# Sharing the first copies, moving adaLN steps off the first two heads, reordering the first FFN weights, spreading two merges, and updating x by ScalarE and GpSimd in a conditioned decoder trunk

## The chip, the core and the metric

The kernel runs on one core of one Trainium2 chip. Its five instruction streams are called by the profile's names: PE (TensorE), DVE (VectorE), ACT (ScalarE), POOL (GpSimd) and SP (the queue from which nearly all DMAs are issued). The metric is the device time of one execution in microseconds; lower is better. Quoted are the median, the lowest and the highest of several runs.

## What is computed

Two residual layers over x (1024 tokens of 1024 channels, f32), each with a mixer and a gated FFN. In front of each of the four blocks stands an RMS norm whose scale and shift come from the conditioning vector c (adaLN), and what a block gives is added to x through a gate that also comes from c:

```python
for i in range(DEPTH):                                   # 2
    mod = (cs @ ada_w[i] + ada_b[i])[:, None, :]         # 1024 x 6144: six vectors of 1024
    sh_m, sc_m, g_m, sh_f, sc_f, g_f = jnp.split(mod, 6, axis=-1)
    hm = rms_norm(x, norm_mix[i]) * (1.0 + sc_m) + sh_m
    y = even_mixer(hm, ...) if i % 2 == 0 else odd_mixer(hm, ...)
    x = x + g_m * y
    hf = rms_norm(x, norm_ffn[i]) * (1.0 + sc_f) + sh_f
    x = x + g_f * conv_ffn(hf, ...)                      # up to 2 x 2816, width-3 conv, silu, down
```

The even mixer (layer 0) is a gated delta rule over 4 heads, with a solve of a triangular system for each chunk of 64 tokens, beside windowed pooling. The odd mixer (layer 1) is dilated sliding-window attention: three groups of 8 heads, whose outputs are merged per head with weights from their softmax denominators, and then an output projection `od_w_out` (1024 x 1024).

## The kernel before

**Products.** x lies transposed in SBUF, as 8 tiles `xr` (or `x`) of 128 channels by 1024 tokens. Each f32 product is three 128x512 matmuls in a row (`mm3`, lines L212 to L214): high weight by high input, high by low, low by high. The parts are called `whi`, `wlo` for a weight, `hh`, `hl` or `oh`, `ol` for an input. A weight granule (`granule`) is one DMA of 256 KB into a `raw` tile, a rounding by ACT into `whi` (L185) and a subtraction into `wlo` (L186), mostly by POOL; nine of each may be alive. A product's sum lies in PSUM, in an `mm` tile (128x1024) or an `sp` tile (128x512). `t2k` is a ring of eight 128x512 tiles in SBUF that many steps share.

**Order.** The program is written as generators. `weave(chain, dense)` lets a chain with long dependences (a norm, a head, an attention unit) yield how many microseconds of dense products are to be put before its next step. A scheduler then fixes each engine's order; it may also put an instruction ahead of others that were written before it where nothing forbids that. `tc.issue_after` forbids it. On the chip each engine then runs its list in order, and waits where the next instruction isn't ready.

**adaLN steps.** `mod` is built in sections of 512 columns of a layer's 6144, so 12 to a layer. A section is eight steps, each a DMA of 256 KB of `ada_w` into a `raw` tile and one accumulation: by DVE (L284, L286), or late in the first FFN by ACT and POOL (L280, L282); then four transposes on PE (L324) and a reduction (L325). Four sections are made at the start from early loads: by PE into one row (`ada_row`, L307) or by DVE (`ada_sum`, L314 and L316). All others come from `step_back`, called at each product: every `pace`-th call makes one step, as long as fewer than `secs_due` sections are done; `sections(n)` makes at once what is missing.

**Stages, by time.** 0 to 65: x is transposed on PE (L552), copied out of PSUM by DVE (L553, 16 copies), its squares summed on ACT (L543), the reciprocal roots made by DVE (L557, L124 to L132) and laid out as rows by PE (L371). 65 to 465: the even mixer; per head `head_keys` (L909), the small inverse (L815 to L838), a transposed copy through DRAM that comes back as `zc`, L954 on DVE, and from L962 on PE the rest of the solve; the short convolutions (L632) are made between these by DVE. 465 to 540: output projection. 540 to 1240: FFN of layer 0, whose start `first_two` runs four units (gate and value of blocks 0 and 1) for one half of the tokens while the other half's norm is made. 1240 to 2240: projections and attention of layer 1, with `qk_norm` (L1400, L1406) and, near 1800, the merges of head pairs 0 and 1 (`merge`: loads L1620, L1622 to L1637 on DVE). 2240 to 2320: the last attention, merges 2 and 3, and the first half of the output projection: `update` with `wide=True` makes 16 products of two halves each for rows 0, 1 and again for rows 2, 3, and DVE adds each to `xr` with L249. 2320 on: the rest of that projection (`edge`) and the second FFN.

Of the kernel before, what the change touches and what calls it, by code (L numbers as in the profile page):

```python
# [34 lines left out]
def trunk(ctx, tc, x, c, ada_w, ada_b, norm_mix, norm_ffn, ev_w_in, ev_w_out, gdn_conv_w,  # L35
# [72 lines left out]
    beat, pace, secs_done, secs_due = [0], [3], [0], [12]  # L108
# [117 lines left out]
    def update(rows, hid, gate, xt, order, wide=False, done=None):  # L226

        wb = []
        for r in rows:
            g = [granule(r[:, q * HALF:(q + 1) * HALF]) for q in range(2)]  # L230
            wb.append([(a, b) for hi, lo in g for a, b in zip(blk4(hi), blk4(lo))])
        n = len(rows)
        ps = None
        for o, hf in order:
            s = HS[hf]
            if wide:
                ps = mm_ps() if hf == 0 else ps
                p = ps[:, s]
            else:
                p = s_ps()  # L240
            for i in range(n):
                mm3(p, wb[i][o], hid[i][hf], i == 0, i == n - 1)
                if i < n - 1:
                    yield 3 * MM
            if not wide:
                nc.vector.scalar_tensor_tensor(out=xt[o][:, s], in0=p, scalar=gate[:, o:o + 1], in1=xt[o][:, s],  # L246
                                               op0=ALU.mult, op1=ALU.add)
            elif hf:
                nc.vector.scalar_tensor_tensor(out=xt[o], in0=ps, scalar=gate[:, o:o + 1], in1=xt[o],  # L249
                                               op0=ALU.mult, op1=ALU.add)  # L250
            if done:
                done(o, hf)
            step_back()
            yield 3 * MM
# [48 lines left out]
    def ada_row(s, raws, ks=range(KT), acc=None):  # L303

        acc = acc or s_ps()
        for k in ks:
            nc.tensor.matmul(acc[:1], cs[:, k:k + 1], raws[s, k], start=(k == 0), stop=(k == KT - 1))  # L307
        return acc
# [58 lines left out]
    def row_of(rs):  # L367

        ps = s_ps()
        for u, d in enumerate(blk4(ps)):  # L370
            nc.tensor.matmul(d, rs[:, u:u + 1].to_broadcast([P, P]), ident, start=True, stop=True)  # L371
        return ps
# [89 lines left out]
    def even():  # L462
# [9 lines left out]
        with tc.tile_pool(name="pe", bufs=1) as pe:  # L472
# [72 lines left out]
            turned = [None]  # L545

            def turn_x(hf):
                for k in range(KT):
                    ps = s_ps()
                    for u, d in enumerate(blk4(ps)):  # L550
                        r = xrs[hf * 4 + u, k // 4]
                        nc.tensor.transpose(d, r[:, k % 4 * P:(k % 4 + 1) * P], ident)  # L552
                    turned[0] = nc.vector.tensor_copy(xt[k][:, HS[hf]], ps)  # L553
# [18 lines left out]
            with tc.issue_after(turned[0].ins):  # L572
                rstd0, rstd1 = rstd_first()
                row8 = ada_row(8, raws)
# [3 lines left out]
            first = units_c(w, (0, 512))  # L578
# [172 lines left out]
            def dense():  # L751
# [13 lines left out]
                with tc.issue_after(res["gt"].ins):  # L765
                    step_back(True)
                    step_back(True)
                for hd in range(1, NH):
                    while ("go", hd) not in ready:
                        yield None  # L770
                    ps = yield from unit(512 + hd * P)
# [343 lines left out]
            sections(12)  # L1115
# [5 lines left out]
    def ffn(l, xt, h, vec, acc, vec_next):  # L1121
        gate = mod[l][:, 40:48]
        wu, wd = ffn_w_up[l], ffn_w_down[l]
        with tc.tile_pool(name=f"pf{l}", bufs=1) as pf:
# [41 lines left out]
            def wu_gate(j):  # L1166
                return unit_c(wu, j * P)

            def wu_val(j):
                return unit_c(wu, DFF + j * P)  # L1170

            def first_two():
# [3 lines left out]
                wb = [wu_gate(0), wu_val(0), wu_gate(1), wu_val(1)]  # L1176
                t = [gate_tile(), gate_tile()]
                d = units([gp, vp, g[1], v[1]], wb, h, (0,))
                weave(norm(xt, vec, h, 1, acc, (4.5, 6.0), keep=True), d)
# [11 lines left out]
                v[1][1] = s_ps()  # L1191
# [103 lines left out]
            if l == 0:  # L1295
                secs_due[0], pace[0] = 24, 14
# [27 lines left out]
    def odd(xt, h, vec, acc):  # L1324
# [5 lines left out]
        with tc.tile_pool(name="po", bufs=1) as po:  # L1330
# [130 lines left out]
            def dense():  # L1461
# [43 lines left out]
                for ks in ((0, 1), (2, 3)):  # L1505
                    upd = update(row_blocks(od_w_out[0], ks), o, gate, res["x"], BY_TILE, wide=True)
# [159 lines left out]
            def chains():  # L1666
                last = len(todo) - 1
                for i in range(last):
                    yield lambda: (i, 0) in ready
                    yield from attend(i, 1.7)  # L1670
                    if i == 5:
                        yield from merge(0, 2.0)
                        yield from merge(1, 2.0)
# [92 lines left out]
```

## Time and profile before

| | before |
|---|---|
| median of 3 runs | 3066.48 us (3061.31 to 3067.76) |
| profiled execution: time | 3061.16 us |
| profiled execution: span | 3059.4 us |
| mean granted TensorE clock | 0.988 |
| busy: PE, DVE, ACT, POOL | 2969.0, 1941.8, 1131.3, 1030.3 us |
| share of the span | 97%, 63%, 37%, 34% |

Busy time is the time in which an engine had an instruction running. A granted clock of 1 is 2.4 GHz, and 0.5 is 1.2 GHz. In the lists of instructions a number in square brackets is the idle time of that engine just before the instruction, and behind the arrow stands what ended it. In the tables by stretch the number in round brackets is a count of instructions.

### The profile page before, as it was taken

What the parts mean: (1) busy time and instruction counts of PE and PEld (TensorE: products, weight loads), DVE (VectorE), ACT (ScalarE), POOL (GpSimd) and SP (SyncE); (2) the same over time, 40 slices, a digit from 0 to 9 for tenths busy, and PEclk for the clock granted to TensorE, in tenths of its full rate; (3) what the DMA queues carried; (4) which work ended last, traced back from release to release, by engine and by line L of the source; (5) the groups of instructions that cost most, each with busy time, mean ns of one, the idle gap of its engine ahead of it and who ended that gap; (6) DMA issues with size and microseconds to landing.
All of it is one profiled execution on the core that took longest, in us unless ns stands there. A gap on an engine that the chain in (4) does not pass through costs nothing.

```text
span 3059.4 us, 40272 instructions
## 1 busy us (share of the span) xinstructions
PE 2969.0 (97%) x14362; PEld 2448.9 (80%) x14362; DVE 1941.8 (63%) x3788; ACT 1131.3 (37%) x2253; POOL 1030.3 (34%) x776
## 2 busy tenths in 40 slices
PE   7999999999999999999999999999999999999999
PEld 4777877778888887888888878888877788888888
DVE  7768745987776655654545646353687776666554
ACT  4434432533334433423333434333344433333210
POOL 3312323565556875200000010000032655556540
PEclk9999999999999999999999999999999999999999
DMA  7423314253323754322224242313253222224321
GB/s 258 138 55 101 104 53 155 79 155 109 110 86 107 235 156 136 133 64 74 91 61 124 69 149 73 108 39 113 68 172 117 83 83 84 84 85 165 111 92 57
DMA packets 274754, 331.46 MB, mean 108 GB/s; under 512 B 27155, under 2 KB 194170, under 8 KB 274554
## 3 DMA queue, kind: packets, MB, share of 16 engines
q1 hardware_dynamic: 266554, 300.54, 31.3%
q0 software_dynamic: 7040, 25.17, 2.4%
q10 hardware_dynamic: 960, 3.18, 0.3%
q8 instruction: 113, 1.85, 0.2%
q14 instruction: 87, 0.71, 0.1%
HBM read 251.82 MB, written 77.00 MB: 107 GB/s over the span
## 4 chain that ended last, share of the span: by engine, by line
PE 75%; DVE 5%; POOL 1%; issue 1%; DMA 1%; ACT 1%; SPq 0%; POOLq 0%; DVEq 0%; ACTq 0%
PE sp L214 12%; PE sp L212 12%; PE sp L213 12%; PE mm L1390 8%; PE mm L1388 8%; PE mm L1389 8%; PE mm L213 3%; PE mm L212 3%; PE mm L214 3%; PE sp L1584 2%; PE sp L1540 2%; PE sp L1420 1%; PE sp L1573 1%; POOL wlo L186 1%; DMA ld<-os 1%
## 5 line engine op out<-in xcount | busy, mean ns | idle before, releaser
L1388 PE MATMUL mm<-whi,hh 128*128 128x512 f32 x1152 | 483.3, 420 | 0.0
L1390 PE MATMUL mm<-whi,hl 128*128 128x512 f32 x1152 | 453.1, 393 | 0.0
L1389 PE MATMUL mm<-wlo,hh 128*128 128x512 f32 x1152 | 451.2, 392 | 0.0
L186 POOL TENSOR_TENSOR wlo<-raw,whi 128x512 fp32r<-128x512 f32 x190 | 259.5, 1381 | 524.8 <-ACT whi L185 456.9
L246 DVE SCALAR_TENSOR_TENSOR xr<-sp,mod,xr 128x512 f32<-128x512 f32 x336 | 251.5, 750 | 182.9 <-PE sp L214 182.8
L185 ACT ACTIVATE whi<-raw 128x512 fp32r<-128x512 f32 x334 | 207.8, 629 | 313.9 <-PE sp L213 99.9
L212 PE MATMUL sp<-oh,whi 128*128 128x512 f32 (+1 forms) x832 | 313.9, 377 | 1.7 <-ACT whi L185 1.7
L214 PE MATMUL sp<-oh,wlo 128*128 128x512 f32 (+1 forms) x832 | 311.8, 375 | 1.5 <-POOL wlo L186 1.3
L213 PE MATMUL sp<-ol,whi 128*128 128x512 f32 (+1 forms) x832 | 311.0, 374 | 0.0
L212 PE MATMUL mm<-hh,whi 128*128 128x512 f32 x704 | 284.7, 406 | 8.3 <-DVE big L632 4.8
L213 PE MATMUL mm<-hl,whi 128*128 128x512 f32 x704 | 280.7, 399 | 1.7 <-DVE hl L397 0.9
L214 PE MATMUL mm<-hh,wlo 128*128 128x512 f32 x704 | 280.1, 398 | 0.0
L186 POOL TENSOR_TENSOR wlo<-t2k,whi 128x512 fp32r<-128x512 f32 x160 | 228.8, 1444 | 148.2 <-ACT whi L185 87.5
L1485 POOL DMA_DIRECT2D vd<-v x24 | 17.6, 735 | 772.2 <-ACT v L1482 380.3
L1390 PEld LDWEIGHTS mm<-whi,hl 128*128 128x128 f32 x1152 | 216.5, 188 | 48.5
L1389 PEld LDWEIGHTS mm<-wlo,hh 128*128 128x128 f32 x1152 | 217.9, 189 | 37.1
L1388 PEld LDWEIGHTS mm<-whi,hh 128*128 128x128 f32 x1152 | 217.4, 189 | 36.0
L186 POOL TENSOR_TENSOR wlo<-wr,whi 128x512 fp32r<-128x512 f32 x114 | 179.5, 1576 | 159.4 <-ACT whi L185 149.9
L214 PEld LDWEIGHTS sp<-oh,wlo 128*128 128x128 f32 x832 | 157.3, 189 | 31.3 <-POOL wlo L186 3.5
L212 PEld LDWEIGHTS sp<-oh,whi 128*128 128x128 f32 x832 | 157.2, 189 | 29.9 <-ACT whi L185 2.9
L213 PEld LDWEIGHTS sp<-ol,whi 128*128 128x128 f32 x832 | 157.3, 189 | 26.8
L212 PEld LDWEIGHTS mm<-hh,whi 128*128 128x128 f32 x704 | 134.0, 191 | 35.9 <-issue 7.8
(392 smaller groups left out, 6231.5 us busy)
## 6 DMA issues: line engine op xcount, KB each, us to landing
raw<-in_ada_w_dram SPq DMA_DIRECT2D x160, 256.0 KB
wr<-in_ffn_w_up_dram SPq DMA_DIRECT2D x76, 512.0 KB
raw<-in_od_w_in_dram SPq DMA_DIRECT2D x144, 256.0 KB
hid<-ft SPq DMA_DIRECT2D x44, 512.0 KB
raw<-in_ffn_w_down_dram SPq DMA_DIRECT2D x88, 256.0 KB
big<-hid SPq DMA_DIRECT2D x44, 512.0 KB
xr<-xs SPq DMA_DIRECT2D x32, 512.0 KB
os<-stg SPq DMA_DIRECT2D x96, 130.0 KB
```

Source lines behind the costliest of these rows:

```text
L185: nc.scalar.activation(dst_hi, src, AF.Copy)
L186: eng.tensor_tensor(out=dst_lo, in0=src, in1=dst_hi, op=ALU.subtract)
L212: nc.tensor.matmul(ps, wh, mh, start=first, stop=False)
L213: nc.tensor.matmul(ps, wh, ml, start=False, stop=False)
L214: return nc.tensor.matmul(ps, wl, mh, start=False, stop=last)
L246: nc.vector.scalar_tensor_tensor(out=xt[o][:, s], in0=p, scalar=gate[:, o:o + 1], in1=xt[o][:, s], op0=ALU.mult, op1=ALU.add)
L1388: nc.tensor.matmul(p, hh, wh, start=(k == 0), stop=False)
L1389: nc.tensor.matmul(p, hh, wl, start=False, stop=False)
L1390: nc.tensor.matmul(p, hl, wh, start=False, stop=(k == KT - 1))
L1420: nc.tensor.transpose(ps[:, (hh * 2 + j) * P:(hh * 2 + j + 1) * P], blk4(qk[j])[s * 2 + hh], ident)
L1540: nc.tensor.matmul(ps[:, at:at + len(ks) * P], qks[i][0][:, hh, blk * P:(blk + 1) * P], qks[i][1][:, hh, ks[0] * P:(blk + 1) * P], start=T ...
L1584: nc.tensor.matmul(ps[:, j * P:(j + 1) * P], pTs[n][:, a0 + c * P:a0 + (c + 1) * P], vb(kb, hh), start=(c == 0), stop=(c == len(ks) - 1))
```

## The change

There are seven edits:

1. In `turn_x`, four of the eight copies of the second half go to ACT.
2. The section made by PE (`ada_row(8, ...)`) is cut in two: four of its eight steps are issued after the transposes and ahead of the rows of reciprocal roots (`row_of`), four behind them.
3. `secs_due` begins at 4 in place of 12 and becomes 10 from head 2 on; two forced steps in head 0 go; the even mixer ends with 10 sections done in place of 12, and the steps of the FFN come every 9th product in place of every 14th.
4. `first_two` loads its four units by halves: the first half of all four, and then the second halves. The first wait of the norm woven into it is 8.0 us of products in place of 4.5. The fourth unit's second half gets an `mm` tile for its sum in place of an `sp` tile.
5. Merge 0 comes after attention unit 5 as before, merge 1 after unit 6.
6. The 32 halves of the updates for rows 0 to 3 of `od_w_out` no longer go through DVE's L249 (16 instructions of 128x1024): ACT scales each half out of PSUM into a `t2k` tile (L250 of the kernel after), and POOL adds it to `xr` (L251 of the kernel after).
7. Names and `last_mm` bookkeeping, for `issue_after`.

```diff
-    beat, pace, secs_done, secs_due = [0], [3], [0], [12]
+    beat, pace, secs_done, secs_due = [0], [3], [0], [4]
...
+            elif wide == "apart":
+                t = t2k()
+                nc.scalar.activation(t, p, AF.Copy, scale=gate[:, o:o + 1])
+                nc.gpsimd.tensor_tensor(out=xt[o][:, s], in0=xt[o][:, s], in1=t, op=ALU.add)
...
-                    turned[0] = nc.vector.tensor_copy(xt[k][:, HS[hf]], ps)
+                    if hf and k % 2:
+                        turned[1] = nc.scalar.copy(xt[k][:, HS[hf]], ps)
+                    else:
+                        turned[0] = nc.vector.tensor_copy(xt[k][:, HS[hf]], ps)
...
-            with tc.issue_after(turned[0].ins):
+            with tc.issue_after(last_mm[0].ins):
+                row8 = ada_row(8, raws, range(4))
+            with tc.issue_after(last_mm[0].ins), tc.issue_after(turned[0].ins):
                 rstd0, rstd1 = rstd_first()
-                row8 = ada_row(8, raws)
+            with tc.issue_after(last_mm[0].ins):
+                ada_row(8, raws, range(4, KT), row8)
...
-            first = units_c(w, (0, 512))
+            with tc.issue_after(turned[1].ins):
+                first = units_c(w, (0, 512))
...
-                with tc.issue_after(res["gt"].ins):
-                    step_back(True)
-                    step_back(True)
                 for hd in range(1, NH):
...
+                    if hd == 2:
+                        secs_due[0] = 10
...
-            sections(12)
+            sections(10)
...
-                wb = [wu_gate(0), wu_val(0), wu_gate(1), wu_val(1)]
+                wb = units_c(wu, (0, DFF, P, DFF + P))
...
-                weave(norm(xt, vec, h, 1, acc, (4.5, 6.0), keep=True), d)
+                weave(norm(xt, vec, h, 1, acc, (8.0, 6.0), keep=True), d)
...
-                v[1][1] = s_ps()
+                v[1][1] = mm_ps()[:, HS[0]]
...
-                secs_due[0], pace[0] = 24, 14
+                secs_due[0], pace[0] = 24, 9
...
-                    upd = update(row_blocks(od_w_out[0], ks), o, gate, res["x"], BY_TILE, wide=True)
+                    upd = update(row_blocks(od_w_out[0], ks), o, gate, res["x"], BY_TILE, wide="apart")
...
-                    if i == 5:
-                        yield from merge(0, 2.0)
-                        yield from merge(1, 2.0)
+                    if i in (5, 6):
+                        yield from merge(i - 5, 2.0)
```

Three places of the engines' lists, before and after; the line numbers of the kernel after are a little higher.

PE behind the last transpose of x, before; `rs` holds the reciprocal roots, `ada` the early loads of `ada_w`:

```order
L552 MATMUL sp_340<-ident,wlo_146 128x128
L371 MATMUL sp_362<-ident,rs_74_347 128x128 x4
L371 MATMUL sp_367<-ident,rs_74_347 128x128 x4
L307 MATMUL sp_372<-ada_152,cs 1x512 x2
L307 MATMUL sp_372<-ada_156,cs 1x512 x2
L307 MATMUL sp_372<-ada_160,cs 1x512 x2
L307 MATMUL sp_372<-ada_164,cs 1x512 x2
```

The same place after:

```order
L556 MATMUL sp_340<-ident,wlo_146 128x128
L311 MATMUL sp_346<-ada_152,cs 1x512 x2
L311 MATMUL sp_346<-ada_156,cs 1x512 x2
L375 MATMUL sp_367<-ident,rs_75_352 128x128 x4
L375 MATMUL sp_372<-ident,rs_75_352 128x128 x4
L311 MATMUL sp_346<-ada_160,cs 1x512 x2
L311 MATMUL sp_346<-ada_164,cs 1x512 x2
```

Half of the section's steps now stand ahead of the rows of reciprocal roots.

DVE in head 0, in the convolution behind `head_keys` and the start of the small inverse, before (L286 is an adaLN step, L632 the convolution, L815, L840, L828 and L831 the inverse):

```order
L632 SCALAR_TENSOR_TENSOR big_1181<-mm_1016,cols,big_1181 128x1022
L286 SCALAR_TENSOR_TENSOR ada_acc_1403<-raw_1454,cs,ada_acc_1403 128x512
L632 SCALAR_TENSOR_TENSOR big_1181<-mm_1016,cols,big_1181 128x1021
L286 SCALAR_TENSOR_TENSOR ada_acc_1403<-raw_1479,cs,ada_acc_1403 128x512
L815 TENSOR_SCALAR t2k_1165<-t2k_1165 64x256
L286 SCALAR_TENSOR_TENSOR ada_acc_1403<-raw_1900,cs,ada_acc_1403 128x512
L840 COPY t2k_1166<-t2k_1165 64x8
L828 TENSOR_TENSOR t2k_1167<-t2k_1165,t2k_1166 64x16
L286 SCALAR_TENSOR_TENSOR ada_acc_1403<-raw_1938,cs,ada_acc_1403 128x512
L828 TENSOR_TENSOR t2k_1165<-t2k_1165,t2k_1166 64x16
L286 SCALAR_TENSOR_TENSOR ada_acc_1403<-raw_1979,cs,ada_acc_1403 128x512
L831 TENSOR_TENSOR t2k_1165<-t2k_1165,t2k_1167 64x16
```

The same place after (L290 is the step, L643 the convolution, L825 to L841 the inverse):

```order
L643 SCALAR_TENSOR_TENSOR big_1140<-mm_992,cols,big_1140 128x1022
L290 SCALAR_TENSOR_TENSOR ada_acc_2112<-raw_2156,cs,ada_acc_2112 128x512
L643 SCALAR_TENSOR_TENSOR big_1140<-mm_992,cols,big_1140 128x1021
L825 TENSOR_SCALAR t2k_1124<-t2k_1124 64x256
L850 COPY t2k_1125<-t2k_1124 64x8
L838 TENSOR_TENSOR t2k_1126<-t2k_1124,t2k_1125 64x16
L838 TENSOR_TENSOR t2k_1124<-t2k_1124,t2k_1125 64x16
L841 TENSOR_TENSOR t2k_1124<-t2k_1124,t2k_1126 64x16
```

Fewer steps stand in it. From the first step to head 0's L954 DVE's list holds 32 steps before and 16 after. The 16 that remain are written from head 2 on and were put forward by the scheduler. On PE 60 dense matmuls stood between the last L944 of head 0 and its first L962; after there are 39.

POOL in the first half of the output projection, before (`wlo` from a weight's `raw`, `ol` from an input):

```order
L186 TENSOR_TENSOR wlo_20079<-raw_20076,whi_20078 128x512
L186 TENSOR_TENSOR ol_19822<-big_19819,oh_19821 128x1024
L186 TENSOR_TENSOR wlo_20085<-raw_20082,whi_20084 128x512
L186 TENSOR_TENSOR ol_19828<-big_19825,oh_19827 128x1024
L186 TENSOR_TENSOR wlo_20091<-raw_20088,whi_20090 128x512
L186 TENSOR_TENSOR wlo_20097<-raw_20094,whi_20096 128x512
L186 TENSOR_TENSOR wlo_20384<-raw_20381,whi_20383 128x512
```

A piece of the same place after, where the first update ends and the second begins:

```order
L251 TENSOR_TENSOR xr_19705<-xr_19705,t2k_20066 128x512
L251 TENSOR_TENSOR xr_19705<-xr_19705,t2k_20075 128x512
L186 TENSOR_TENSOR wlo_20136<-raw_20133,whi_20135 128x512
L251 TENSOR_TENSOR xr_19706<-xr_19706,t2k_20093 128x512
L186 TENSOR_TENSOR wlo_20463<-raw_20460,whi_20462 128x512
L186 TENSOR_TENSOR wlo_20469<-raw_20466,whi_20468 128x512
L186 TENSOR_TENSOR wlo_20475<-raw_20472,whi_20474 128x512
L251 TENSOR_TENSOR xr_19706<-xr_19706,t2k_20112 128x512
L251 TENSOR_TENSOR xr_19699<-xr_19699,t2k_20146 128x512
```

The 32 adds (L251) now stand in POOL's list between the splits.

## Rows read from the trace of the kernel before

**Rows 1.** Busy time by stretch, columns: stretch, its length, then busy time (and count) of PE, PEld (weight loads), DVE, ACT and POOL, the granted clock, the DMA share and GB/s.

```profile
615.00:1190.00 575.00, 572.27 (x2540) 473.39 (x2539) 409.37 (x490) 221.16 (x314) 368.47 (x246) 1.00 0.44 138
2240.00:2320.00 80.00, 71.33 (x344) 57.98 (x343) 69.81 (x188) 35.37 (x100) 25.01 (x18) 0.94 0.57 187
```

**Rows 2.** What PE waited for over the whole span: us in total, times, longest us.

```profile
PE sp L962 <- DVE g L954: 7.4, 2, 7.2
PE mm L212 <- DVE xr L249: 5.8, 4, 4.3
PE sp L1420 <- DVE t2k L1406: 4.8, 2, 4.5
PE sp L1584 <- DVE sb L1575: 4.0, 3, 3.0
```

**Rows 3.** The opening in order of time: the copies of x on DVE and the last step of the reciprocal roots, then PE; columns: start, duration, engine, line, operation, tile, count, and in brackets the idle time before.

```profile
16.80 4.27 DVE L553 COPY x<-sp 128x512 f32<-128x512 f32 x7
23.41 0.17 DVE L132 SCALAR_TENSOR_TENSOR rs<-rs,rs 128x8 f32<-128x8 f32 x1
...
23.72 3.63 PE L371 MATMUL sp<-ident,rs 128*128 128x128 f32 x16 [4.33 <-DVE rs L132]
27.28 7.03 PE L307 MATMUL sp<-ada,cs 128*1 128x512 f32 x16
39.60 0.80 PE L212 MATMUL mm<-hh,whi 128*128 128x512 f32 x1 [2.83 <-DVE hh L396]
```

**Rows 4.** Head 0: the adaLN steps on DVE from 100 to 175 us as one group, the gaps of PE, dense matmuls at the full clock, and the stretches around (columns as in Rows 1).

```profile
L286 DVE SCALAR_TENSOR_TENSOR ada_acc<-raw,cs,ada_acc 128x512 f32<-128x512 f32 x28 | 25.2, 898 | 3.7 <-DMA raw<-in_ada_w_dram 3.5
...
129.99 0.39 PE L213 MATMUL mm<-hl,whi 128*128 128x512 f32 x1
134.97 0.39 PE L214 MATMUL mm<-hh,wlo 128*128 128x512 f32 x1
140.61 0.77 PE L212 MATMUL mm<-hh,whi 128*128 128x512 f32 x1 [3.67 <-DVE big L632]
172.71 1.09 PE L962 MATMUL sp<-ident,g 128*128 128x128 f32 x4 [7.21 <-DVE g L954]
...
120.00:140.00 20.00, 16.94 (x81) 13.85 (x79) 18.93 (x37) 5.70 (x22) 6.88 (x6) 1.00 0.57 169
140.00:147.00 7.00, 6.39 (x24) 5.80 (x25) 3.34 (x9) 2.58 (x3) 1.27 (x1) 0.52 0.73 202
173.00:178.00 5.00, 4.83 (x25) 4.36 (x24) 1.94 (x2) 1.17 (x2) 0.69 (x1) 0.55 0.36 105
```

**Rows 5.** The starts of the two FFNs: the gaps of PE at the first, DVE's wait for PE there, and stretches of both (columns as in Rows 1).

```profile
559.61 0.50 PE L212 MATMUL sp<-hh,whi 128*128 128x512 f32 x1 [1.66 <-ACT whi L185]
563.09 0.75 PE L214 MATMUL sp<-hh,wlo 128*128 128x512 f32 x1 [2.52 <-POOL wlo L186]
...
567.48 0.69 DVE L325 TENSOR_REDUCE rs<-sp 128x4 f32<-128x512 f32 x1 [2.21 <-PE sp L324]
...
563.00:567.00 4.00, 3.91 (x11) 3.10 (x12) 2.27 (x2) 0.01 (x1) 3.40 (x3) 0.57 0.44 126
575.00:615.00 40.00, 37.93 (x168) 31.09 (x167) 39.78 (x56) 25.33 (x40) 29.33 (x17) 1.00 0.15 46
2372.00:2379.00 7.00, 5.13 (x14) 4.15 (x15) 3.47 (x3) 1.80 (x3) 5.18 (x4) 0.52 0.37 117
```

**Rows 6.** The end of the first FFN: POOL's splits behind its last adaLN accumulation, what PE waited for from 1190 to 1210 us, and the stretch behind (columns as in Rows 1).

```profile
1195.38 8.95 POOL L186 TENSOR_TENSOR wlo<-raw,whi 128x512 fp32r<-128x512 f32 x7
...
PE sp L212 <- ACT whi L185: 1.7, 3, 0.8
PE sp L214 <- POOL wlo L186: 1.3, 2, 0.7
...
1201.00:1208.30 7.30, 6.15 (x13) 3.92 (x13) 1.43 (x3) 3.00 (x5) 4.56 (x4) 0.53 0.74 222
```

**Rows 7.** The merges: the longest wait of DVE, the gap of PE, and the stretch after it (columns as in Rows 1).

```profile
1813.54 0.16 DVE L1622 TENSOR_REDUCE mx<-ld 128x2 f32<-128x6 f32 x1 [6.99 <-DMA ld<-os]
...
1818.46 0.33 PE L1420 MATMUL sp<-ident,t2k 128*128 128x128 f32 x1 [4.54 <-DVE t2k L1406]
...
1819.00:1823.00 4.00, 3.94 (x14) 3.41 (x15) 3.35 (x15) 1.00 (x3) 0.00 (x0) 0.57 0.43 121
```

**Rows 8.** The output projection from 2240 to 2320 us: groups of DVE and POOL (count, busy us, mean ns, idle before), two single merge steps of DVE with POOL's instruction of that time, and for prices an add and a PSUM copy from elsewhere in the span (the copy: shortest, median and longest ns).

```profile
L1637 DVE SCALAR_TENSOR_TENSOR t2k<-ld,me,t2k 128x128 f32<-128x128 f32 x56 | 23.4, 463 | 1.9 <-ACT t2k L1635 1.7
L249 DVE SCALAR_TENSOR_TENSOR xr<-mm,mod,xr 128x1024 f32<-128x1024 f32 x15 | 19.2, 1279 | 1.8 <-PE mm L214 1.8
L186 POOL TENSOR_TENSOR wlo<-raw,whi 128x512 fp32r<-128x512 f32 x16 | 21.0, 1330 | 33.5 <-ACT whi L185 31.7 <-DVE rr L132 1.8
...
2275.46 2.30 DVE L1637 SCALAR_TENSOR_TENSOR t2k<-ld,me,t2k 128x128 f32<-128x128 f32 x1 [1.34 <-ACT t2k L1635]
2279.03 0.34 DVE L1637 SCALAR_TENSOR_TENSOR t2k<-ld,me,t2k 128x128 f32<-128x128 f32 x1
2275.21 2.40 POOL L186 TENSOR_TENSOR ol<-big,oh 128x1024 fp32r<-128x1024 f32 x1 [0.33 <-PE sp L1584]
...
L186 POOL TENSOR_TENSOR ext<-xr,ext 128x512 fp32r<-128x512 f32 x8 | 12.9, 1626 | 0.0
L1399 ACT ACTIVATE t2k<-mm x96: 572/597/619, 1307.5 to 2252.0; 128x512 f32<-128x512 f32 x96
```

More of the change, by code (lines that the diff above doesn't have):

```diff
@@ L306, in ada_row @@
         for k in ks:
-            nc.tensor.matmul(acc[:1], cs[:, k:k + 1], raws[s, k], start=(k == 0), stop=(k == KT - 1))
+            last_mm[0] = nc.tensor.matmul(acc[:1], cs[:, k:k + 1], raws[s, k], start=(k == 0), stop=(k == KT - 1))
         return acc
@@ L370, in row_of @@
         for u, d in enumerate(blk4(ps)):
-            nc.tensor.matmul(d, rs[:, u:u + 1].to_broadcast([P, P]), ident, start=True, stop=True)
+            last_mm[0] = nc.tensor.matmul(d, rs[:, u:u + 1].to_broadcast([P, P]), ident, start=True, stop=True)
         return ps
@@ L543, in even @@
                     nc.scalar.activation(t2k(), xrs[t, q], AF.Square, accum_out=ssx[:, t, q:q + 1])
-            turned = [None]
+            turned = [None] * 2
             def turn_x(hf):
@@ L551, in turn_x @@
                         r = xrs[hf * 4 + u, k // 4]
-                        nc.tensor.transpose(d, r[:, k % 4 * P:(k % 4 + 1) * P], ident)
-                    turned[0] = nc.vector.tensor_copy(xt[k][:, HS[hf]], ps)
+                        last_mm[0] = nc.tensor.transpose(d, r[:, k % 4 * P:(k % 4 + 1) * P], ident)
+                    if hf and k % 2:
+                        turned[1] = nc.scalar.copy(xt[k][:, HS[hf]], ps)
+                    else:
+                        turned[0] = nc.vector.tensor_copy(xt[k][:, HS[hf]], ps)
             def rstd_first():
@@ L1164, in ext @@
                 return pf.tile([P, T], dt, tag="ext", name=nm(name), bufs=8)
[L1166 to L1170, printed above, removed]
             def first_two():
```

## Prediction

> **What bounds the kernel now.** The first view to read is the page's busy times: PE works 2969.0 of 3059.4 us, so it is the bound nearly everywhere. PE's matmuls are the same before and after. What the change can win is PE's idle time, 3059.4 - 2969.0 = 90 us over all, and the time in which the granted clock is at 0.5. The second view is the list of PE's waits: it names what ended each gap, and the largest entries lie where the change works [rows 2]. The third is the table by stretch, which tells where PE idles and who is full there: from 615 to 1190 us PE idles only 2.7 us, from 2240 to 2320 us 8.7 us, with DVE busy 69.8 of 80 [rows 1]. The fourth is the order of time around each gap. It shows a second cost: behind the gap that ends at 140.61 the granted clock is 0.52 for 7 us, and a matmul that starts every 0.226 us at the full clock ((134.97 - 129.99) / 22) takes nearly twice that [rows 4]. A stretch at half clock thus loses about half its length, on top of the gap. That happens behind nearly every gap of 3 us or more here, and behind groups of smaller ones [rows 4 to 7].
>
> The sums are made against the profiled execution, 3061.2 us (1.8 around a span of 3059.4). It lies 5.3 below the median, 3066.5, so the result is moved up by 5.3 at the end.
>
> **Part by part.**
>
> *Opening.* DVE's copies take 4.27 / 7 = 0.61 us each; four fewer on its way bring the reciprocal roots from 23.6 to 21.2, and ACT, idle there since it finished the squares, takes four copies of some 0.6. PE's half section (7.03 / 2 = 3.5 us) fills most of its 4.33 us gap, and the other half follows the rows [rows 3]. The first product at 39.6 waits 2.83 us for DVE's `hh`, though, so it is DVE's list that has to come sooner. The 2.4 us of copies are the gain I take, with bounds of 0 (the weights or later `ada_w` loads are late instead) and 4 (the whole PE gap). **-2.4.**
>
> *Head 0.* DVE loses 16 of 32 steps ahead of L954: 16 x 0.898 = 14.4 us, and half of 3.7 us of waiting for their loads, together 16 [rows 4]. DVE is busy 18.93 of 20 us there, so its chain to L954 moves by about that. But 21 dense matmuls that stood ahead of L962 now stand behind it: PE has 21 x 0.226 = 4.7 us less to do while it waits. DVE-bound, the gain is 16 - 4.7 = 11.3. PE-bound, it is all that goes: gaps of 3.67 and 7.21, 7 x 0.48 = 3.4 and 5 x 0.45 = 2.2 at half clock [rows 4], together 16.5. The lower bound is 4: the chain also holds a round trip of PE products and a transfer, which steps off DVE don't shorten. I take the middle one, as DVE is the full engine. **-11.** The two sections that leave the mixer reappear in the first FFN: 16 steps of 0.9 are 14 us on a DVE busy 409 of 575 us, where PE idles 2.7 [rows 1]. Cover is there; if it fails at one step in five, 3 us. **+1.**
>
> *FFN starts.* The second half of a fourth unit comes too late because its granules wait for the ring of nine; PE idles 1.66 and 2.52 us, and loses 4 x 0.43 = 1.7 at half clock, 5.9 in all; in the second FFN the same place loses 7 x 0.48 = 3.4 at half clock, and I take the same 4.2 us of gaps for it [rows 5]. By halves, five free granules serve the first half of all four units. But DVE is busy 39.78 of 40 us from 575 to 615: what PE wins is paid back unless DVE gets its work earlier. DVE waits 2.21 us for the transposes behind those gaps [rows 5]. These transposes gain 5.9 and lose 18 matmuls put ahead of them by the longer wait, 18 x 0.226 = 4.1: 1.8 us. Bounds 0 and 5.9 for the first, 0 and 7.6 for the second; between them I take a little more than the 1.8, 2.5 and 3.5, since the tail of the chain also has ACT and POOL in it. **-6.**
>
> *End of the first FFN.* POOL makes seven splits in 8.95 us without a break while PE waits 3.0 us for them and then loses 7.3 x 0.47 = 3.4 [rows 6]. Steps that come every 9th product leave eight steps in place of eleven to be made at once ahead of these splits. An add on POOL of that form takes 1.3 (a split takes 8.95 / 7 = 1.28), so the splits come 3 x 1.3 = 3.9 us sooner. Bounds 0 (the loads set the pace) and 6.4. **-3.**
>
> *Merges.* DVE sits 6.99 us in L1622 for a load; `qk_norm`'s L1406 stands behind it, and PE waits 4.54 and loses 4 x 0.43 = 1.7 [rows 7]. Apart, the second merge has an attention unit in front of it, in which its loads can land. Bounds: -6.2 and +1, as it can meet a late load again behind unit 6. **-5.**
>
> *Updates.* From 2240 to 2320 DVE loses 16 x 1.279 = 20.5 us. ACT gets 32 copies of about 0.6 (the median is 597 ns), 19 us on an engine busy 35 of 80. POOL gets 32 adds. The nearest rows are a split, 1.33, and an add of x of the same size, 1.626: 43 to 52 us, on an engine busy 25 of 80 [rows 1, 8]. PE idles 80 - 71.3 = 8.7 us in this stretch and loses 80 x 0.06 = 4.8 to the clock, 13.5 together: without gaps it would need 66.5. POOL would need 43 + 2 x 2.40 + 21.0 for the splits = 69, with the dearer adds 78. So POOL becomes about the bound, and the edit is worth 80 - 69 = 11 to 80 - 78 = 2. Next, the price of company: a merge step of DVE takes 0.34 alone, and 2.30 when POOL's 2.40 us instruction runs beside it [rows 8]. The 56 steps average 0.463, 0.12 above; with POOL busy 68 of 80 rather than 25, that would be 0.12 x 2.7 x 56 = 18 us (estimate from these rows) of the 20.5 won. What stays is that `mm` is emptied by ACT and not behind DVE's queue. I take a value nearer to the dearer adds, as their row is also an add of x; the other bound is a loss of 8, a fourth of POOL's 31.7 us of waiting for `whi` coming on top of 78 [rows 8]. **-4.**
>
> The Trainium skill, page "SBUF — State Buffer", section "Who interferes with whom", speaks against this edit: a DVE instruction with two SBUF inputs contends with a GpSimd instruction that reads SBUF, and one of them blocks whole, while L249, with one input in PSUM, would not contend. By that rule POOL's new adds hold up the merge steps and are held up by them; the trace agrees, with 2.30 against 0.34 us. By it the edit's worth would be about 0, and the sum 4 us less.
>
> Sum: 2.4 + 11 - 1 + 6 + 3 + 5 + 4 = 30.4. 3061.2 - 30.4 = 3030.8, as a median 3036.
>
> **The rivals.**
>
> 1. *Given back.* What PE wins at the opening, the FFN starts and the end of the FFN shows up again as waits for DVE further on, and the updates win nothing. For it speaks DVE's 39.78 of 40 us [rows 5]; against it that PE's waits have different releasers [rows 2]. Head 0 with 8 and the merges with 5 stay: 3066.5 - 13 = 3053.
> 2. *POOL sets the end of the updates; slower.* Each add stands in POOL's list behind splits, and POOL already waits 31.7 us there for ACT's `whi` [rows 8]. ACT in turn holds a `t2k` tile until the add is done and then can't empty `mm`. With adds of 1.626 and all these waits kept POOL needs 52 + 4.8 + 21 + 31.7 = 110 us, and if each of the 56 merge steps holds POOL for its 0.34 us, as POOL held them, 129 in place of 80: +49. It ends slower as soon as POOL's list takes over 80 + 26 + 6 = 112 us there (the other parts give 26). For it: one list in order, four engines in a circle. Against it: most of the 31.7 is slack, not waiting that delays anyone. 3066.5 - 26 + 49 = 3090.
> 3. *The steps don't leave head 0 in effect.* 16 of them stay in front of L954; if the round trip, not DVE, sets L954, the gap moves with PE and only some 2 us are won. 3066.5 - 21 = 3045.
> 4. *All gaps go.* The upper bounds of all parts together are 4 + 16.5 + 13.5 + 6.4 + 6.2 + 11 = 58; if nine tenths hold, 3014.
>
> **How the numbers follow.** Chances: forecast (3024 to 3043) 0.45, rival 1 0.20, rival 2 0.10, rival 3 0.10, rival 4 0.12, no change worth measuring for other reasons 0.03. The likeliest is 3036. The range leaves out rival 2 and the far end of rival 4: 3014 to 3059. About 0.2%, 6 us, is what a measurement tells from no change. Faster: 0.45 + 0.12 + 0.10 + most of rival 1 = 0.83; within 0.2%: the rest of rival 1 and the 0.03, 0.07; slower: 0.10.
>
> **What would show it.** In the profile after: no PE gap over 3 us and no clock of 0.5 from 19 to 28 us; L962's first wait under 2 us and the clock at 1 from 140 to 147; no wait for `whi` and `wlo` of the fourth unit, with DVE's wait for L324 shorter; less than 1 us of gaps near 1197; no wait of L1622 over 3 us followed by one of L1420; in the stretch that was 2240 to 2320 POOL busy 69 to 78 us, and L1637's mean above 0.463. The prediction falls if L962 still waits 5 us or more, if the gaps behind the FFN starts grow by what was won ahead of them, or if PE waits for `mm` tiles that ACT empties late because POOL's adds are late.

## The result and the profile after

| | before | after |
|---|---|---|
| median of 10 runs each | 3063.57 us | 3073.91 us (3068.5 to 3080.83) |
| ratio, with 95% interval | 1 | 1.0037 (1.0025 to 1.0049) |
| span of the profiled execution | 3059.4 us | 3066.5 us |
| busy: PE, DVE, ACT, POOL | 2969.0, 1941.8, 1131.3, 1030.3 us | 2961.2, 1946.5, 1148.7, 1056.6 us |

The change made the kernel 0.37% slower; the prediction was about 1% faster. The first step is to see where the time goes. The same instruction is looked up in both traces (start in us):

| instruction | before | after | after - before |
|---|---|---|---|
| first product | 39.60 | 39.15 | -0.5 |
| 63rd matmul of L1026 (L1036 after), near the end of the solve | 475.56 | 470.00 | -5.6 |
| 21st L1155 (L1159) on ACT, inside the first FFN | 980.06 | 976.40 | -3.7 |
| first L1420 (L1424), layer 1 | 1314.04 | 1303.43 | -10.6 |
| 361st L1420 (L1424), ahead of the updates | 2225.54 | 2214.93 | -10.6 |
| first L371 (L375) of the second FFN's norm | 2352.68 | 2359.23 | +6.6 |
| 31st L1281 (L1285) on ACT, inside the second FFN | 2620.78 | 2628.04 | +7.3 |

In this pair of traces the kernel after is 10.6 us ahead until 2215 us. It then loses 17.9 us, 17.2 of them ahead of the second FFN's norm: in the updates.

The loss is clear, the lead less so. Ten kept traces have DVE's updates, and from the 361st L1420 to the 31st L1281 they take 392.1 to 396.6 us (395.2 before, 413.1 after). But the start of layer 1 differs by more than that among kernels that are the same up to there: seven with the code of after reach it between 1303.4 and 1318.6 us, 1311.2 in the mean, and four with the code of before between 1312.0 and 1319.3, 1315.1 in the mean. So the lead is about 4 us, and the 10.6 are in part the luck of this pair.

The tables of the stretch of the updates say how the loss comes about. The stage is the one of [rows 1], 2240 to 2320 before; it takes longer after, so 117 us are shown. First the busy times of the kernel after by stretch (columns as in rows 1):

```profile
2228.00:2250.00 22.00, 14.64 (x83) 12.54 (x84) 20.38 (x65) 11.61 (x33) 9.04 (x7) 0.89 0.77 275
2250.00:2280.00 30.00, 25.54 (x113) 20.15 (x113) 19.11 (x38) 16.78 (x41) 21.23 (x15) 0.85 0.45 150
2280.00:2308.00 28.00, 23.12 (x113) 17.83 (x111) 11.13 (x10) 16.18 (x34) 24.90 (x20) 0.98 0.24 76
2308.00:2345.00 37.00, 32.60 (x133) 24.34 (x134) 28.90 (x84) 16.10 (x41) 13.39 (x10) 0.92 0.38 119
```

PE idles 117 - 95.9 = 21 us in these 117 (80 - 71.3 = 8.7 in the 80 before), and the clock is below 1 in all four stretches. No engine is full over the whole of it, not even POOL, with 68.6 of 117: DVE is full first (20.4 of 22), then POOL (24.9 of 28, while DVE has 11.1), then DVE again has most of the work. The engines take turns, and PE waits for each. DVE's merge steps and POOL's adds, from 2225 to 2345 us (count, busy us, mean ns, idle before):

```profile
L1641 DVE SCALAR_TENSOR_TENSOR t2k<-ld,me,t2k 128x128 f32<-128x128 f32 x56 | 33.1, 643 | 8.3 <-ACT t2k L1639 8.2
L251 POOL TENSOR_TENSOR xr<-xr,t2k 128x512 f32<-128x512 f32 x32 | 41.4, 1319 | 17.4 <-ACT t2k L250 9.4 <-DMA ld<-os 4.1 <-issue 3.9
```

A merge step takes 0.643 us in the mean, 0.463 before [rows 8]. What PE waited for in these 117 us (us in total, times, longest):

```profile
PE sp L1647 <- DVE t2k L1641: 8.3, 4, 5.4
PE sp L1424 <- DVE t2k L1410: 7.0, 1, 7.0
PE mm L212 <- ACT t2k L250: 4.9, 2, 4.1
```

None of these stood in [rows 2] for that place. Of those that did, the wait for L249 is gone, and that for L1575 (L1579 after) is small. L1647 is the transpose of a merged tile. The longest of the waits for it, in order of time, with DVE, POOL and PE:

```profile
2301.34 6.57 DVE L1641 SCALAR_TENSOR_TENSOR t2k<-ld,me,t2k 128x128 f32<-128x128 f32 x1 [7.22 <-ACT t2k L1639]
...
2296.58 7.52 POOL L251 TENSOR_TENSOR xr<-xr,t2k 128x512 f32<-128x512 f32 x6
2304.03 1.29 POOL L186 TENSOR_TENSOR wlo<-raw,whi 128x512 fp32r<-128x512 f32 x1
2305.25 2.51 POOL L251 TENSOR_TENSOR xr<-xr,t2k 128x512 f32<-128x512 f32 x2
...
2308.59 0.45 PE L1647 MATMUL sp<-ident,t2k 128*128 128x128 f32 x1 [5.40 <-DVE t2k L1641]
```

One merge step of DVE, 0.34 us when alone [rows 8], stands from 2301.34 to 2307.91, as long as POOL runs adds and splits without a break, and ends 0.15 us behind the last of them (2305.25 + 2.51 = 2307.76). PE gets its tile 0.7 us later. The third wait has the same start, and shows how it reaches ACT:

```profile
2262.43 6.46 DVE L1641 SCALAR_TENSOR_TENSOR t2k<-ld,me,t2k 128x128 f32<-128x128 f32 x4
2270.94 0.15 DVE L1567 TENSOR_SCALAR neg<-stg 128x2 f32<-128x2 f32 x1
...
2271.12 0.51 ACT L1569 ACTIVATE sb<-sb,neg 128x256 f32<-128x256 f32 x1 [5.22 <-DVE neg L1567]
...
2274.72 0.80 PE L212 MATMUL mm<-whi,whi 128*128 128x512 f32 x1 [4.06 <-ACT t2k L250]
```

Four merge steps take 6.46 us (1.46, 1.37, 2.48 and 1.37) while POOL again works without a break. L1567 stands behind them on DVE, ACT sits 5.22 us in front of L1569 for it, and behind L1569 in ACT's list stand the copies (L250) that empty `mm`. PE waits 4.06 us for one. The second wait, 7.0 us for L1410, has another cause: no add of POOL runs ahead of it (the first starts at 2247.90, when L1410 is under way). The section on the held transposes comes back to it.

The other places. In the opening ACT's copy of the row stands behind four roundings, of which the last is shown:

```profile
31.34 0.63 ACT L185 ACTIVATE whi<-raw 128x512 fp32r<-128x512 f32 x1 [0.24 <-DMA raw<-in_ev_w_in_dram]
31.88 0.56 ACT L335 COPY t2k<-sp 1x512 f32<-1x512 f32 x1
...
32.49 0.58 PE L337 MATMUL sp<-ident,t2k 1*128 1x1 f32 x4 [4.42 <-ACT t2k L335]
39.15 1.22 PE L212 MATMUL mm<-hh,whi 128*128 128x512 f32 x2 [2.98 <-DVE hh L400]
```

PE had its sums 6.4 us earlier (it stands idle from 28.07), and the first product is 0.5 us earlier than in [rows 3] (38.9 in the mean of the seven traces named above, 40.1 in that of the four). At head 0, the steps of DVE as one group, and PE, to be read beside [rows 4]:

```profile
L290 DVE SCALAR_TENSOR_TENSOR ada_acc<-raw,cs,ada_acc 128x512 f32<-128x512 f32 x14 | 13.8, 984 | 7.2 <-DMA raw<-in_ada_w_dram 7.1
...
161.34 1.09 PE L972 MATMUL sp<-ident,g 128*128 128x128 f32 x4 [3.72 <-DVE g L964]
```

Half the steps are gone, but those that are left wait 7.2 us for their loads in place of 3.7. At the start of the first FFN, PE's waits from 540 to 640 us, beside [rows 5]:

```profile
PE sp L212 <- DVE ft L1282: 5.8, 1, 5.8
PE mm L213 <- DVE hl L401: 2.6, 2, 1.4
PE sp L375 <- DVE rs L132: 1.6, 1, 1.6
```

The waits for `whi` and `wlo` are gone. The wait for L1282 (L1278 before), which was 2.7 us, is 5.8. At the end of the first FFN POOL's splits, beside [rows 6]:

```profile
1186.44 3.81 POOL L186 TENSOR_TENSOR wlo<-raw,whi 128x512 fp32r<-128x512 f32 x3
1190.51 6.33 POOL L186 TENSOR_TENSOR wlo<-raw,whi 128x512 fp32r<-128x512 f32 x5 [0.26 <-ACT whi L185]
```

The first starts 8.9 us earlier than before, 3.7 of it the lead that the kernel has at 980 us in this pair. PE waits once from 1190 to 1212 us, 0.8 us. At the merges DVE and PE wait as in [rows 7]:

```profile
1803.38 0.16 DVE L1626 TENSOR_REDUCE mx<-ld 128x2 f32<-128x6 f32 x1 [7.58 <-DMA ld<-os]
...
1808.14 2.35 PE L1424 MATMUL sp<-ident,t2k 128*128 128x128 f32 x8 [5.24 <-DVE t2k L1410]
```

### The profile page after: what moved, and what is told of

It is laid out like the page before. It is cut to its first block, busy times and chain, and to the rows that moved or that the text cites. A ratio compares the mean times of both kernels' runs of the same rounds, so it can differ in the third digit from the quotient of the medians.

```text
span 3066.5 us, 40355 instructions
## 1 busy us (share of the span) xinstructions
PE 2961.2 (97%) x14362; PEld 2439.3 (80%) x14362; DVE 1946.5 (63%) x3770; ACT 1148.7 (37%) x2285; POOL 1056.6 (34%) x807
## 4 chain that ended last, share of the span: by engine, by line
PE 67%; DVE 8%; POOL 3%; DMA 3%; issue 3%; ACT 1%; SPq 0%; POOLq 0%; ACTq 0%; DVEq 0%
PE sp L212 9%; PE sp L214 9%; PE sp L213 9%; PE mm L1394 8%; PE mm L1392 8%; PE mm L1393 8%; PE mm L212 3%; PE mm L213 3%; PE mm L214 3%; PE sp L1588 2%; PE sp L1544 2%; PE sp L1424 1%; POOL ada_acc L286 1%; POOL wlo L186 1%; DVE t2k L1641 1%
## 5 line engine op out<-in xcount | busy, mean ns | idle before, releaser
L186 POOL TENSOR_TENSOR wlo<-raw,whi 128x512 fp32r<-128x512 f32 x190 | 249.8, 1329 | 477.8 <-ACT whi L185 431.2
L213 PEld LDWEIGHTS mm<-hl,whi 128*128 128x128 f32 x720 | 136.2, 189 | 38.0 <-DVE hl L401 9.2
```

The source lines that it names most:

```text
L186: eng.tensor_tensor(out=dst_lo, in0=src, in1=dst_hi, op=ALU.subtract)
L213: nc.tensor.matmul(ps, wh, ml, start=False, stop=False)
```

## The experiments

Each run is compared with runs of the kernel before on the same chip; the ratio is to these. Single executions of one kernel spread by some 10 us, so differences below 3 us are taken from medians with care. The price of the stage of the updates (361st L1420 to 31st L1281) is taken from the traces, where it is good to some 3 us, as said above.

**The updates back on DVE (e1).**

```diff
-upd = update(row_blocks(od_w_out[0], ks), o, gate, res["x"], BY_TILE, wide="apart")
+upd = update(row_blocks(od_w_out[0], ks), o, gate, res["x"], BY_TILE, wide=True)
```

> The kernel after with the updates of rows 0 to 3 put back on DVE (wide=True), all else as after. Theory A (the adds on POOL cost what the rest won): the stretch from 2240 us loses about 20 us less, so 10 to 12 us faster than before, near 3053 with a median of before of 3064. Theory B (the loss is in the other edits or in the merges, and the updates are about even): within 4 us of the kernel after, near 3074.

Measured: 3056.43 us, ratio 0.9976 (0.9965 to 0.9986). Theory A, though with less than its 10 to 12 us: the rest of the change is worth about 8 us (4 to 11 by the interval), and the updates cost more than that. In its trace the stage of the updates takes 1.4 us more than before, in place of 17.9.

**The updates by ACT and POOL alone (e2).** The kernel before with the new branch of `update` and `wide="apart"`.

> The kernel before with the updates by ACT and POOL alone. Theory A: 16 to 20 us slower than before, near 3081, with merge steps of over 1 us on DVE where POOL's adds run. Theory B: within 4 us of before, near 3064.

Measured: 3082.19 us, ratio 1.0057 (1.0041 to 1.0073), 17.4 us. The cost is there without any other edit. The merge steps from 2225 to 2345 us average 0.673 us, against 0.460 before in the same window:

```profile
L1641 DVE SCALAR_TENSOR_TENSOR t2k<-ld,me,t2k 128x128 f32<-128x128 f32 x55 | 34.4, 673 | 8.2 <-ACT t2k L1639 8.1
```

**Adds beside DVE's updates (e9).** The kernel before, with 32 adds on POOL that nothing needs (the call has `wide="beside"`):

```diff
+                if wide == "beside":
+                    for q in HS:
+                        nc.gpsimd.tensor_tensor(out=t2k(), in0=xt[o][:, q], in1=xt[o][:, q], op=ALU.add)
```

> The kernel before, with 32 adds of 128x512 on POOL beside its 16 updates on DVE; each reads a half of xr and writes a t2k tile that nobody reads. Nothing waits for their values. Theory A1 (POOL's reads of SBUF hold up DVE's merge steps): L1637's mean rises well above 0.463 us and the kernel is 8 to 15 us slower. Theory A2 (the detour of the update itself over ACT, t2k and POOL is what costs): within 3 us of before.

Measured: 3074.07 us, ratio 1.0042 (1.003 to 1.0054). DVE's merge steps and POOL's adds in it, from 2225 to 2345 us:

```profile
L1640 DVE SCALAR_TENSOR_TENSOR t2k<-ld,me,t2k 128x128 f32<-128x128 f32 x60 | 30.9, 564 | 0.1
...
L253 POOL TENSOR_TENSOR t2k<-xr 128x512 f32<-128x512 f32 x32 | 33.2, 1060 | 24.5 <-DVE xr L249 13.2 <-DVE mx L1625 4.6 <-DVE rr L132 3.0
```

Adds that nobody reads, somewhat shorter ones (1.06 us), cost 13.5 us by the medians and 10.8 in the stage: theory A1. The detour of the update isn't needed for a loss of this size; POOL's work at that place is enough. These adds also take `t2k` tiles and places in POOL's list, so the 10.8 isn't only DVE held up; that part shows in the 0.564 us.

**The adds on DVE (e5).** The kernel after, with one line changed:

```diff
-nc.gpsimd.tensor_tensor(out=xt[o][:, s], in0=xt[o][:, s], in1=t, op=ALU.add)
+nc.vector.tensor_tensor(out=xt[o][:, s], in0=xt[o][:, s], in1=t, op=ALU.add)
```

> The kernel after with ACT still scaling each half out of PSUM, but the 32 adds on DVE (both inputs in SBUF) in place of POOL. Theory A1 (POOL's adds hold up DVE's merge steps, and DVE then holds up ACT): most of the loss goes, 3054 to 3060, though DVE has 32 adds of some 0.7 us. Theory A2 (it is ACT's part that costs: 32 copies in ACT's queue ahead of the attention's exponentials, and the t2k ring): the loss stays, 3070 or more.

Measured: 3062.99 us, ratio 0.9996 (0.9986 to 1.0007). Theory A1, with a rest: the stage costs 6.4 us more than before in place of 17.9. Moving the same adds to a DVE that is fuller wins 11 us, and a merge step there takes 0.420 us. DVE's groups, and PE's waits, from 2225 to 2345 us:

```profile
L251 DVE TENSOR_TENSOR xr<-xr,t2k 128x512 f32<-128x512 f32 x32 | 25.7, 811 | 13.8 <-ACT t2k L250 13.5
L1641 DVE SCALAR_TENSOR_TENSOR t2k<-ld,me,t2k 128x128 f32<-128x128 f32 x56 | 20.4, 420 | 0.1
...
PE sp L1424 <- DVE t2k L1410: 7.0, 1, 7.0
PE mm L212 <- ACT t2k L250: 5.2, 5, 1.8
```

The wait for a merge step, 8.3 us in the kernel after, is gone, and the longest wait for an `mm` tile is 1.8 in place of 4.1. The wait for L1410 stands as it was, without an add on POOL.

**Half of the tiles by POOL (x7).** The kernel after with `elif wide == "apart" and o % 2:`, the other tiles by L249.

> The kernel after with every second tile's updates on DVE by L249, so 16 adds on POOL in place of 32. If the cost goes with the number of POOL's adds: half of the 17 us, near 3064. If it is a threshold (POOL full, back to back adds that lock DVE out for several in a row): much less than half, near 3058.

Measured: 3068.6 us, ratio 1.0019 (1.0008 to 1.003). In the traces the stage costs 6.9 us with 16 adds, against 1.4 with none and 17.9 with 32. By the ratios the first 16 adds cost more than the second: 0.9976, 1.0019, 1.0037. So half of the adds cost a third (traces) to seven tenths (ratios) of the whole. That speaks for a cost by the add and against a threshold that spares the first half; which half is dearer isn't shown.

**The transposes held (a2, e5b).** The 7.03 us wait of L1424 seemed to have a cause in PE's list. In the kernel after no dense matmul stands between that place's L1577 and the first L1424; before there were 18 behind the first of the matching L1573, and PE waited there too, 4.3 us for L249 [rows 2].

```diff
-                        if turn:
-                            run_turn(1)
+                        if turn:
+                            with tc.issue_after(last_mm[0].ins):
+                                run_turn(1)
```

> The kernel after, with the last transposes of q and k on PE (L1424) held behind the update's products, so that 24 dense matmuls stand between L1577 and the first of them, where 0 stood in the kernel after and 18 before the change. Theory A (part of the loss is PE's list: L1424 stands at the front and waits 7.03 us for DVE): 5 to 9 us faster than the kernel after, near 3066; what is left is POOL's. Theory B (the wait only moves to mm, which ACT empties late): within 3 us of the kernel after, near 3074.

Measured: 3076.82 us, ratio 1.0051 (1.0038 to 1.0064). And with the adds on DVE:

> ACT scales out of PSUM, DVE adds, and the transposes are held as in a2. With DVE's adds the updates cost 6 us more than L249, and the trace has the same 7.03 us wait of L1424. Theory A: that wait and its half clock are the 6 us; held, 4 to 8 us faster than with DVE's adds alone, near 3056. Theory B (ACT's copies or the second pass on DVE cost the 6 us): no faster, near 3062.

Measured: 3065.35 us, ratio 1.0018 (1.0009 to 1.0027). Theory A fell in both: nothing was won, and e5b is even slower than e5 (0.9996). PE's waits in the first of the two, from 2225 to 2345 us:

```profile
PE mm L212 <- ACT t2k L250: 11.1, 3, 6.3
PE sp L1648 <- DVE t2k L1642: 5.8, 2, 5.3
```

The wait for L1410 is gone, and one of 6.3 us for an `mm` tile stands in its place: ACT's first L250 stands in ACT's list behind roundings that wait for DVE, as L249 stood behind `qk_norm` on DVE before. So emptying `mm` on ACT doesn't free it of DVE. What exactly the remaining 6 us of e5 consist of stays open.

**The two merges together again (e4)**, on top of the updates by DVE.

> The kernel after with the updates back on DVE and merge 1 back behind merge 0. Against the run with only the updates back it prices the merges. If merge 0 alone meets the late loads, moving merge 1 wins nothing: the same time within 3 us. If the two merges in a row were the trouble, as the prediction had it, 5 us slower.

Measured: 3061.33 us, ratio 0.9984 (0.9973 to 0.9995), against 0.9976 for e1 with overlapping intervals: moving merge 1 alone wins nothing that can be told.

**Merges one unit later (x3, y1)**, after units 6 and 7, with the opening of e8 below:

```diff
-                    if i in (5, 6):
-                        yield from merge(i - 5, 2.0)
+                    if i in (6, 7):
+                        yield from merge(i - 6, 2.0)
```

> The opening of e8 and updates on DVE, with merges 0 and 1 after attention units 6 and 7 in place of 5 and 6. In every run so far merge 0 after unit 5 waits 7 us for a load while POOL's eight loads of v run, and PE loses 4.5 to 5.2 us to it and a stretch at half clock. Theory A (the place after unit 5 is what collides): no such wait, 5 to 6 us faster than e8, near 3049. Theory B (a merge meets such loads after any unit): the wait moves, within 3 us of e8.

Measured: 3046.65 us, ratio 0.9955 (0.9943 to 0.9967). Theory A, and more than it asked: DVE doesn't wait for `ld` there, and PE has no wait at all from 1770 to 1900 us. The same edit alone on the kernel before:

> The kernel before with one edit: merges 0 and 1 after attention units 6 and 7. x3, which has this and others, was 14 us faster than before. Theory A (the place of merge 0 alone is worth the wait near 1813, 4.54 us, and the half clock behind it, 1.7, or somewhat more): 6 to 10 us faster than before. Theory B (it needs the other edits): no more than 3 us faster.

Measured: 3055.93 us, ratio 0.9974 (0.9961 to 0.9986). It is worth some 8 us by itself (4 to 12 by the interval). In its trace 5.9 us of that lie between the first and the 361st L1420, which it covers in 905.6 us, the kernel before in 911.5.

**The row's copy first (e8).** In e1, the four first granules are loaded as before, but their roundings are written behind ACT's copy of the row (`row_copy`):

```diff
+            with tc.issue_after(row_copy[0].ins):
+                for n, r in enumerate(first_raw):
+                    ...
+                    split(hi, lo, r, lo_eng[0])
```

> The kernel after with the updates back on DVE, and ACT's copy of the adaLN row put ahead of the roundings of the first four weight granules in ACT's list. In the trace after PE idles 4.42 us for that copy, which stands behind four roundings that wait for weights until 31.3 us. Theory A (ACT's order holds the opening): the first product comes 2 to 3 us earlier, and so does the end. Theory B (the weights or the later loads of ada_w hold it): no difference.

Measured: 3054.82 us, ratio 0.9981 (0.9972 to 0.9991), which can't be told from e1's. The opening itself is plain in the trace, PE of this kernel:

```profile
29.01 0.40 PE L338 MATMUL sp<-ident,t2k 1*128 1x1 f32 x4 [0.52 <-ACT t2k L336]
...
35.46 1.22 PE L213 MATMUL mm<-hh,whi 128*128 128x512 f32 x2 [4.48 <-DVE hh L401]
```

The first product comes at 35.46, 3.7 us ahead of the kernel after and 4.1 ahead of before. In x3 and y2, which have the same opening, it comes at 35.19 and 35.94. So that part holds; the medians are too coarse to show it at the end.

**The adaLN steps alone (e6)**: edit 3 on the kernel before.

> The kernel before with edit 3 alone (adaLN steps off heads 0 and 1, and their new pace in the FFN). The trace after has L972 (L962 before) 11.4 us earlier, but 21 dense matmuls (4.8 us) stand behind it that stood ahead of it. Theory A (the 11.4 already hold all that DVE gives, so 4.8 go off them): 6 to 9 us faster than before, the end of the FFN's splits with it. Theory B (the prediction's 11 and 3 were won, and lost again by the other edits): 13 to 15 us faster. Theory C (the steps that fill heads 2, 3 and the FFN take it back): no difference.

Measured: 3055.2 us, ratio 0.9985 (0.9974 to 0.9997), 5 us; between theory A and nothing, and not the 13 of theory B. Its trace, of one of its slowest executions (3065.6 us), doesn't show where they are won.

**The old start of the FFNs**, three times: the new start (edit 4) taken out of e1 (e7), taken out of x3 (y2), and put alone on the kernel before (y3).

> The kernel after with the updates back on DVE and the start of both FFNs as before. PE idled 9.0 us from 555 to 630 before and 10.0 after. Theory A (what the halves win at the fourth unit is waited for again at the first sums for block 2, which DVE delivers): within 3 us of the run with only the updates back, near 3056. Theory B (the prediction's 6 us were won): 6 us slower than that run, near 3062.

Measured: 3057.94 us, ratio 0.9996 (0.9985 to 1.0008).

> x3 with the start of both FFNs as before. By x3's trace the new start is won early and waited for again: 6.71 us for the first sums of block 2 in the second FFN, where before it was 3.73. Theory A (the start is worth nothing): within 3 us of x3, 3044 to 3050. Theory B (it is worth the prediction's 6 us): 6 us slower than x3.

Measured: 3051.42 us, ratio 0.996 (0.9946 to 0.9975).

> The kernel before with edit 4 alone, the first four units of both FFNs by halves. Theory A: within 3 us of before, with the waits for whi and wlo of the fourth unit gone and the waits for L1278's sums longer by as much. Theory B (prediction): 6 us faster.

Measured: 3065.54 us, ratio 1.0008 (0.9998 to 1.0018). The first comparison alone would have spoken for 6 us (0.9976 to 0.9996). The other two, one of them the edit by itself, give none. PE's waits in the last, 540 to 640 us:

```profile
PE sp L212 <- DVE ft L1278: 5.7, 1, 5.7
PE sp L371 <- DVE rs L132: 2.9, 1, 2.9
PE mm L213 <- DVE hl L397: 2.8, 2, 1.5
```

They sum to 11.4 us. Before, the four waits of that stretch were 1.66 and 2.52 [rows 5], and 2.1 and 2.7 for `ft`: 9.0. All three are waits for DVE now: theory A.

## Why the prediction was wrong

The step that failed first is the term for the updates, -4, which measured +17.9 in the stage. The prediction saw the price of company, a merge step of 2.30 us beside a POOL instruction, and spread it as a mean over DVE's busy time: 18 us, covered by the 20.5 that DVE lost. The mean rose by less than that, 56 x (0.643 - 0.463) = 10 us. What it left out is where the delay lies. It falls on the one merge step that PE or ACT is waiting for, up to 6.57 us at once. DVE, ACT and POOL each have a list in order, so that a delay on one is a delay for what stands behind it on the next. DVE's freed time stands elsewhere: it had 11.1 of 28 us to do while PE still idled. POOL's busy time, forecast at 69 to 78, was 68.6 in the 117 us, and did not bind as a sum either.

Of the 17.9, some 11 go with the adds' place on POOL: e5 takes them away by moving the adds, and e9 makes 10.8 by adds alone. The rest, 6.4 us in e5, isn't POOL's. Whether ACT's copies or DVE's second pass make it stays open, but the prediction put no cost down for it: that ACT and not DVE's queue empties `mm` was its gain. Its own sign against itself, PE waiting for `mm` tiles that ACT empties late, was there with 4.9 us, though it was DVE that held ACT, not POOL's adds. Rival 2 had the right direction and a circle of engines, with too large a price (+49) and too small a chance, 0.10.

The updates are not the whole miss. The other parts were forecast at 26.4 us, and e1, which has only them, is 8 us faster than before (4 to 11).

The rule of the Trainium skill, "SBUF — State Buffer", section "Who interferes with whom", was given 4 us, because its effect was set against DVE's busy time. The traces agree with it, and more plainly after than before: a step of 0.34 us takes 6.57 and ends 0.15 us after POOL's train does. The same page, section "SBUF: two separate sides", says that the shared pair is locked for a whole instruction by whoever starts first. By that alone a step would wait for one instruction of 1.3 us. The four steps at 2262.43 fit that: three took 1.37 to 1.46 us, and one 2.48 beside a subtraction of 2.44. The one at 2301.34 waited through five, without getting in between.

The other terms, by their steps:

- *Opening, -2.4:* -0.5 in this pair, -1.2 in the means. DVE's list came sooner as said, and PE's sums by 6.4, but the copy between them stands on ACT behind roundings that wait for weights, which the prediction had named only as "the weights". PE's gap only moved behind its sums, and the granted clock is 0.51 from 30 to 44 us. With the copy first the term is 4.1.
- *Head 0, -11:* 5.6 at the end of the solve in this pair, and nothing in the means: eight traces with after's code start the 63rd L1036 at 473.4 us (469.0 to 479.9), five with before's code the 63rd L1026 at 473.5 (472.5 to 475.6). L972 came 11.4 us earlier, not 16, since the steps that stay wait 7.2 us for their loads in place of 3.7. The dense matmuls that no longer stand ahead of it go off that, as worked out. They are made between the first L972 of head 1 and that of head 3, where there are 155 + 174 in place of 143 + 159: 27 x 0.226 = 6.1 us, and the lead falls from 11.0 to 4.9 there. Why still less is left in the means stays open; for the whole of edit 3, e6 gives 5 by its medians.
- *More steps in the FFN, +1:* 1.9 lost between 475 and 980 in this pair, with the FFN's start in it, and nothing clear in the means.
- *FFN starts, -6:* none. Rival 1 was right in this part. The prediction had worked out 1.8 us for DVE, and took a value above it.
- *End of the first FFN, -3:* about 7 between 980 and 1314 in this trace, 3.9 in that of e1, 4.6 in the means. Right, with POOL's first split 8.9 - 3.7 = 5.2 us sooner, against the 3.9 of the sum.
- *Merges, -5:* none. The late load and its price were read rightly, but it is merge 0 that meets it, and the edit moved merge 1. With both one unit later, the step is worth 8.

## What to carry to other kernels

Work that is moved to POOL must be priced by what DVE has to do at the same time with two inputs in SBUF, and by who waits for those very steps, not by either engine's busy time. When a wait is moved, look at what stands in front of it in the list of the engine that takes it over: emptying a PSUM tile on ACT rather than on DVE won nothing while ACT itself waited for DVE. A lead read from one pair of traces needs a look at how much kernels with the same code differ at that place. And where a load comes late, move the first one that collides: one unit later for both merges was worth more than every other part of this change (x3, with updates on DVE, 14 us faster than before, is the best version found).

## What was not expected of the hardware

A DVE instruction of two SBUF inputs can fail to get in between back to back instructions of POOL: 6.57 us in place of 0.34, through five of them, though at other times such a step waited for about one. Why it is the one or the other was not tried. And POOL's adds hardly suffer: their mean is 1.319 us in the kernel after (1.27 to 1.95), against 1.33 for a split of the same size before [rows 8], while DVE's merge steps went from 0.463 to 0.643.
